# Seven small edits to the order of a decoder step: prefetch and scaling of x, a pinned subtraction, a store on another queue, a pause at the key head's change

## The chip, the cores and the metric

The program runs on one core of one Trainium2 chip. The metric is the time of one execution in microseconds on the device. A lower number is better.

## The reference

One inference step of a one-layer decoder with two groups of heads, for a prompt of 1024 tokens and eight further sequences of one token each (R = 1032 rows), all in float32:

```python
h = rmsnorm(x); p = project(h, w_in)          # 2048 wide; q, k, v, index q/k/w, gates, mLSTM q/k/v/i/f/o/z
att = dsa(p.q, p.k, p.v, p.qi, p.ki, p.wi)    # an indexer scores all keys, the 256 best are attended; 8 heads, 2 key heads
h_ml = mlstm(p.mq, p.mk, p.mv, p.ig, p.lf)    # gated linear recurrence, 4 heads, d_v 256, d_qk 128
a  = att * silu(p.az)
mo = rmsnorm_per_head(h_ml) * ml_norm_w * sigmoid(p.mo) * silu(p.mz)
y  = rmsnorm(x + concat(a, mo) @ w_out)
```

The eight further tokens read paged caches of 4096 earlier tokens through a page table (keys, values and index keys) and update stored mLSTM states. Returned are y for both parts, the new keys, values and index keys, and the mLSTM states.

## The kernel before

The matrix products are made of pairs of short floats: each operand is split into a high part H (a cast, on ACT) and a low part L (operand minus H, on DVE), and three products H·H, H·L and L·H are summed on TensorE (PE). So behind each weight tile stand a DMA load on SP, a cast on ACT (`wH`), a subtraction on DVE (`wL`), and PE.

The input projection walks over column blocks, numbered T = 0 to 60. T below 9 are the indexer's and other small parts, T = 9 to 16 the mLSTM values (line 1590), up to 36 the remaining ones (line 1520). From T_G = 37 the gates follow in pairs of column blocks (line 1757), as a Strassen scheme: quarters of x are summed in advance, into DRAM (`xsD`), and so are weights (`usD`). The output projection is again Strassen-like: a first part at line 2040, then sums of weight quarters and products at line 2107 (the tail of the program, from 1714 us on).

Beside the projections run side jobs, written as Python generators and handed out by three lanes. A job has an earliest start and a due time, both in units of T, and a weight, and each `yield w` says how much of the weight was done. The lane takes steps from a job so that it ends at its due time. `prep` makes the sums of x on POOL (`xsD`), `dscore` scores the cached index keys (it fetches rows `kp` by an indirect DMA on POOL, line 1001, and multiplies at line 1023), `att` is the attention of the prompt, `ml` the mLSTM.

The order on each engine comes from a planner that orders the instructions after a model of their times. An instruction that is wrapped in `pin` keeps its place in the program's order; `tc.high_priority()` lets one go ahead; all others may be moved within their dependencies. So a change of a job's due time reorders PE, DVE, ACT and SP over long stretches. Each engine's queue, and each engine's queue of DMA issues, works in order.

The names at the seven places:

- `job_att`: `load_k` loads the transposed keys of a key head into `kL` (line 583, from `akS`), ACT casts `kH` (584), DVE subtracts (585); in the trace these two tiles are named xL and xH. `scores` are the products at 637, `values` those at 681 and 690, `split_q` prepares queries. There are two key heads with 16 pairs of query blocks each; between the 16th and the 17th the key head changes.
- `job_ml`: `main` computes two heads of a chunk of 128 tokens (lines 843 to 920; products of CH with qH and qL at 892), `tail` transposes their rows on PE, copies them to `hT` (one buffer, line 930) and stores them to `hS` (line 931). `load` brings `rb` (831) and `qkv` (834).
- `job_prep`: for each of 16 steps `load` brings four quarters of x (1397), two multiplications for each of two halves scale them (1408 by the norm's weight `nw`, 1409 by `rstd`), three subtractions and an addition make the sums (1412 to 1415), two DMAs store them (1416, 1417). All of it is pinned on POOL.
- The tail: `sP4`, `sP7`, `sP5`, `sP3` are split sums of the quarters `quad(k)` of the activations (2017 and 2018 make sH and sL, 2171 is the subtraction a22 - a11, 2288 the later one, quad(k)[1] - quad(k)[3]). `tsplit` makes wH and wL (2091, 2096), `tsum` sums weights on POOL or DVE (2101), `add` adds products to `yt` (2221).

Of the kernel before, what the change touches and what calls it, by code (L numbers as in the profile page):

```python
# [8 lines left out]
F32 = mybir.dt.float32  # L9
# [43 lines left out]
T_AZ = 53  # L53
NT = 61
T_PA = 55.5
T_PRE = 58
HR = R // 2
CS = HR // 2
NP = (NT - T_G) // 2
# [112 lines left out]
def body(tc, A, stop=None):  # L172
# [65 lines left out]
    def bank(n=512, dt=F32, parts=128):  # L238
        t = psg.tile([128, 512], F32, name="bank")
        return t  # L240
# [328 lines left out]
    def job_att():  # L569
# [4 lines left out]
        with tc.tile_pool(name="at", bufs=2) as pa:  # L574
# [131 lines left out]
            for n, pair in enumerate(pairs):  # L706
                g, i, hp = pair
                nxt = pairs[n + 1] if n + 1 < len(pairs) else None
                ga, gb = groups(pair)
                now["oT"] = bank()  # L710
                if nxt:
                    if nxt[0] != g:
                        load_k(nxt[0])
                    if nxt[2] == 0:
                        split_q(*pre)
                        if n + 3 < len(pairs):
                            pre = load_q(*blocks[(n + 1) // 2 + 1])
                    new = start()
                    scores(nxt, 0, new)
                values(pair, now, ga)  # L720
                if nxt and nxt[0] != g:
                    vt = load_v(nxt[0])
                yield cost[n]
                if nxt:
                    scores(nxt, 1, new)
                    soft(nxt, new)
                values(pair, now, gb)
                V.reciprocal(cur["rc"][:, hp * 2:hp * 2 + 2, i], now["sv"][:, :, 3])
                ob = pa.tile([128, 2, 128], F32, name="ob", bufs=1)
                SC.copy(ob, now["oT"][:, :256].rearrange("p (a b) -> p a b", a=2))  # L730
                SY.dma_start(attS[g].rearrange("(j p) r -> p j r", p=128)[:, hp * 2:hp * 2 + 2, i * 128:(i + 1) * 128],
                             ob)
                if nxt is None or nxt[0] != g:
                    p = bank()
                    PE.transpose(p[:32, :128], cur["rc"].rearrange("p h i -> p (h i)"), ident)
                    rt = pa.tile([128, 512], F32, name="pP", bufs=6)[:32, :128]
                    V.tensor_copy(rt, p[:32, :128])
                    SY.dma_start(rcS[g].rearrange("h (i p) -> (h i) p", p=128), rt)
                if nxt:
                    if nxt[0] != g:  # L740
                        split_v(vt)
                    now = new
                yield cost[n]
# [67 lines left out]
    def job_ml():  # L811
        gT = mlc["gT"]
        with tc.tile_pool(name="ml", bufs=2) as pm:
# [109 lines left out]
            def tail(c, h0, hms):  # L923
                tsl = slice(c * 128, (c + 1) * 128)
                pH = bank().rearrange("p (a b) -> p a b", a=4)
                for hh in range(2):
                    for x in range(2):
                        PE.transpose(pH[:, hh * 2 + x, :], hms[hh][:, x * 128:x * 128 + 128], ident)
                hT = pm.tile([128, 4, 128], F32, name="hT", bufs=1)
                SC.copy(hT, pH)  # L930
                SY.dma_start(hS.rearrange("(j p) r -> p j r", p=128)[:, 2 * h0:2 * h0 + 4, tsl], hT)

            steps = [(c, h0) for c in range(8) for h0 in (0, 2)]
            ld = [load(*steps[0])]
# [454 lines left out]
    def job_prep():  # L1389
        with tc.tile_pool(name="sx", bufs=2, side="right") as px:  # L1390
            halves = rstd.rearrange("p (h t) -> p h t", h=2)
            steps = [(k, c) for k in range(8) for c in range(0, HR, CS)]

            def load(k, c):
                X = px.tile([128, 2, 2, CS], F32, name="X")
                for y in (1, 0):
                    pin(G.dma_start(X[:, y], A["xT"][k + 8 * y].rearrange("p (h t) -> p h t", h=2)[:, :, c:c + CS]))
                return X

            Xs = [load(*steps[0])]  # L1400
            yield 1
            for n, (k, c) in enumerate(steps):
                X = Xs.pop(0)
                if n + 1 < len(steps):
                    Xs.append(load(*steps[n + 1]))
                a11, a21, a12, a22 = (X[:, y, h] for y in range(2) for h in range(2))
                for y in (1, 0):
                    pin(G.tensor_scalar(X[:, y], X[:, y], nw[:, k + 8 * y:k + 8 * y + 1], None, OP.mult))
                    pin(G.tensor_tensor(X[:, y], X[:, y], halves[:, :, c:c + CS], OP.mult))
                yield 1  # L1410
                O = px.tile([128, 3, CS], F32, name="O")
                pin(G.tensor_tensor(O[:, 0], a21, a22, OP.subtract))
                pin(G.tensor_tensor(O[:, 2], a11, a21, OP.subtract))
                pin(G.tensor_tensor(O[:, 1], O[:, 0], a11, OP.subtract))
                pin(G.tensor_tensor(a12, a12, O[:, 1], OP.add))
                pin(G.dma_start(xsD[2:5, k, :, c:c + CS].rearrange("n p t -> p n t"), O))
                pin(G.dma_start(xsD[0:2, k, :, c:c + CS].rearrange("n p t -> p n t"), X[:, 1]))
                yield 1
# [34 lines left out]
    def ix_weight(blocks):  # L1453
# [5 lines left out]

    lanes = [Lane([Job("gates", 5, T_MV - 0.5, 8500, job_gates),  # L1460
                   Job("index", T_MV, 32.5, 3000 + sum(map(ix_weight, groups)), lambda: job_index(groups)),
                   Job("att", T_MQ, T_G + 11.5, 2 * 2 * sum(2 * (1 + (i + 1) * 0.5) for i in range(8)) + 14, job_att, att_free),
                   Job("ml", T_G + 8, T_PRE - 0.75, 39, job_ml)]),
             Lane([Job("prep", 3, T_MV + 5.5, 1 + 16 * 2, job_prep),
                   Job("dscore", T_MV + 6, 21.5, 24 + 128 + 2, job_dscore),
                   Job("dsel", T_MV, 30.5, 2000 + 31 * 1700 + 10000 + 16 * 2800 + 2000, job_dsel),
                   Job("qrows", T_MQ + 0.5, 31, 1, job_qrows),
                   Job("datt", T_MQ, T_G + 0.5, 10000 + 8 * 5000 + 34000 + 5 * 2500 + 8000 + 8000 + 5000, job_datt, ix_free),
# [806 lines left out]
    for n in range(2):  # L2275
        ps = banks3(n)
        for k in range(8):
            with tc.high_priority():
                b22 = wblock(1, 2 + n, k, pt, 6)
                b12 = wblock(0, 2 + n, k, *((wst, 2) if k % 2 else (pt, 6)))  # L2280
                T_ = tsplit(tsum(b22, b12, G), None, True)
            blocks(ps, k, sP7[k], T_, LOW)
            spread(3)
            if not n:
                with tc.high_priority():
                    sP5[k] = ssplit(quad(k)[2])
            if n:
                V.tensor_tensor(quad(k)[1], quad(k)[1], quad(k)[3], OP.subtract)
        for b in LOW:
            late.append(add(yt[b + HB][2 + n], ps[b], yt[b][2 + n]))  # L2290
            late.append(add(yt[b + HB][n], ps[b], yt[b + HB][n]))
        rows3(resid, HIGH, n, False)
        rows3(square, HIGH, n)
        rows3(resid, LOW, 2 + n, False)
        rows3(scaled, HIGH, n)
# [121 lines left out]
```

## Time and profile before

| | |
|---|---|
| median of three runs | 1970.5 us (1966.37 to 1972.38) |
| profiled execution | 1974.54 us, span of its instructions 1972.7 us |
| mean granted clock of TensorE | 0.993 |
| busy: PE, PEld, DVE, ACT, POOL | 1917.7, 1820.3, 1433.6, 900.2, 508.5 us |
| DMA | 421.31 MB, mean 214 GB/s |

The busy times are shares of the span of one execution; PEld is the loading of weights into TensorE, which runs beside the products. Stages by time: 0 to 176 us loading and the first columns, 176 to 390 the mLSTM values, 390 to 932 the columns up to T = 36, 932 to 1617 the gates, then the output projection until the end. A granted clock below 1 means that TensorE was slowed for a while.

### The profile page before, as it was taken

To read this page: it belongs to the slowest core of one execution; us is meant where nothing else is said; L and a number is where in the kernel's file an instruction comes from. 1 tells how busy PE (TensorE), PEld (TensorE's weight loads), DVE (VectorE), ACT (ScalarE), POOL (GpSimd) and SP (SyncE) were. 2 spreads that over 40 slices of the span, in tenths; PEclk is the share of its full clock that TensorE was granted. 3 is DMA by queue.
4 is the path that set the end of the run, shared out by engine and by line. 5 is a ranking of instruction groups with operands and counts; after the bars stand their busy time and mean duration, and the time that the engine had idled before them with its cause. 6 is when DMAs were issued, how large, how long until landed. Compare 5 with 4: busy or idle time off the path is not lost.

```text
span 1972.7 us, 35929 instructions
## 1 busy us (share of the span) xinstructions
PE 1917.7 (97%) x12710; PEld 1820.3 (92%) x12710; DVE 1433.6 (73%) x3280; ACT 900.2 (46%) x1864; POOL 508.5 (26%) x566
## 2 busy tenths in 40 slices
PE   9999999999999999999999999999999999998997
PEld 9998877899999999999999999999999999976885
DVE  8443878676868878975556658777778676788786
ACT  8122554445314454311345546555656434454545
POOL 0576777022311011042000000002123221106633
PEclk9999999999999999999999999999999999999999
DMA  7567556456998687575533687759789858898875
GB/s 262 143 201 201 168 170 186 119 143 199 261 250 228 176 210 209 136 223 191 162 98 113 210 282 207 239 181 280 226 279 316 216 204 291 265 322 284 267 239 187
DMA packets 250289, 421.31 MB, mean 214 GB/s; under 512 B 40101, under 2 KB 117221, under 8 KB 246269
## 3 DMA queue, kind: packets, MB, share of 16 engines
q1 hardware_dynamic: 217709, 328.80, 53.1%
q0 software_dynamic: 18432, 82.15, 15.7%
q10 hardware_dynamic: 13968, 8.06, 1.4%
q8 instruction: 100, 1.64, 0.4%
q14 instruction: 80, 0.66, 0.1%
HBM read 333.76 MB, written 135.48 MB: 238 GB/s over the span
## 4 chain that ended last, share of the span: by engine, by line
PE 75%; DMA 10%; DVE 8%; issue 3%; ACT 2%; SPq 1%; POOL 1%; ACTq 0%; POOLq 0%; DVEq 0%
PE pj L1520 24%; PE pj L1757 18%; PE pj L2107 5%; PE bank L2040 4%; PE bank L1757 3%; PE bank L489 3%; PE bank L637 2%; PE bank L690 2%; PE pj L1590 2%; PE bank L1520 2%; PE bank L681 1%; PE bank L1023 1%; DMA wraw<-in_wv_dram 1%; DVE wL L2096 1%; DMA spD<-ev 1%
## 5 line engine op out<-in xcount | busy, mean ns | idle before, releaser
L1520 PE MATMUL pj<-xH,wH 128*128 128x344 f32 (+1 forms) x1200 | 388.6, 326 | 5.3 <-DVE ev L375 1.9
L1520 PE MATMUL pj<-xH,wL 128*128 128x344 f32 (+1 forms) x1200 | 388.4, 324 | 1.2 <-DVE wL L252 1.2
L1520 PE MATMUL pj<-xL,wH 128*128 128x344 f32 (+1 forms) x1200 | 388.3, 324 | 0.2 <-DVE xL L309 0.2
L1757 PE MATMUL pj<-xH,xL 128*128 128x258 f32 x1152 | 328.1, 285 | 0.0
L1757 PE MATMUL pj<-xH 128*128 128x258 f32 x1152 | 327.9, 285 | 0.0
L1757 PE MATMUL pj<-xL,xH 128*128 128x258 f32 x1152 | 327.8, 285 | 0.0
L1520 PEld LDWEIGHTS pj<-xH,wH 128*128 128x128 f32 x1200 | 225.8, 189 | 8.6 <-issue 2.8
L1520 PEld LDWEIGHTS pj<-xH,wL 128*128 128x128 f32 x1200 | 226.1, 188 | 2.5 <-DVE wL L252 1.5
L1520 PEld LDWEIGHTS pj<-xL,wH 128*128 128x128 f32 x1200 | 226.0, 188 | 1.6 <-DVE xL L309 0.4
L251 ACT CAST wH<-wraw 128x512 fp32r<-128x512 f32 (+2 forms) x183 | 109.6, 610 | 258.3 <-PE pj L1520 161.5
L1757 PEld LDWEIGHTS pj<-xL,xH 128*128 128x128 f32 x1152 | 218.2, 189 | 1.3
L1757 PEld LDWEIGHTS pj<-xH 128*128 128x128 f32 x1152 | 218.3, 190 | 1.0 <-issue 0.4
L1757 PEld LDWEIGHTS pj<-xH,xL 128*128 128x128 f32 x1152 | 218.1, 190 | 1.0
L252 DVE TENSOR_TENSOR wL<-wraw,wH 128x512 fp32r<-128x512 f32 (+2 forms) x183 | 129.0, 715 | 74.4 <-ACT wH L251 71.9
L538 ACT ACTIVATE eq<-eq 128x512 bf16<-128x512 bf16 (+2 forms) x93 | 78.5, 844 | 129.5 <-DVE eq L537 129.2
L2107 PE MATMUL pj<-wL,sH 128*128 128x512 f32 x336 | 127.0, 397 | 8.2 <-DVE wL L2096 8.2
L2107 PE MATMUL pj<-wH,sH 128*128 128x512 f32 x336 | 132.5, 395 | 1.3 <-ACT wH L2091 1.1
L2107 PE MATMUL pj<-wH,sL 128*128 128x512 f32 x336 | 131.7, 392 | 0.0
L491 ACT ACTIVATE rl<-bank 128x512 f32<-128x512 f32 (+2 forms) x160 | 80.5, 524 | 97.7 <-PE bank L489 50.1
L494 DVE SCALAR_TENSOR_TENSOR s<-rl,wiN,s 128x512 f32<-128x512 f32 (+2 forms) x150 | 100.4, 689 | 21.2 <-ACT rl L491 18.8
L882 POOL CAST aH<-onec 128x4 fp32r<-128x4 f32 x16 | 5.5, 343 | 405.8 <-DVE onec L821 405.8
L2107 PEld LDWEIGHTS pj<-wL,sH 128*128 128x128 f32 x336 | 63.7, 190 | 24.2 <-DVE wL L2096 11.0
(511 smaller groups left out, 4817.9 us busy)
## 6 DMA issues: line engine op xcount, KB each, us to landing
wraw<-in_wt_dram SPq DMA_DIRECT2D x144, 256.0 KB
wraw<-in_wa_dram SPq DMA_DIRECT2D x110, 256.0 KB
usD<-in_wa_dram POOLq DMA_DIRECT2D x48, 512.0 KB, 7.6
wraw<-in_wo_dram SPq DMA_DIRECT2D x64, 256.0 KB
usD<-in_wa_dram SPq DMA_DIRECT2D x24, 512.0 KB
usD<-usD POOLq DMA_DIRECT2D x24, 512.0 KB, 5.9
xL<-xsD SPq DMA_DIRECT2D x40, 258.0 KB
ev<-spD SPq DMA_DIRECT2D x38, 258.0 KB
```

Of the source, the lines that this page charges most:

```text
L251: a = SC.copy(H[:, s, :cols], raw[:, s, :cols])
L252: return a, V.tensor_tensor(L[:, s, :cols], raw[:, s, :cols], H[:, s, :cols].bitcast(F32), OP.subtract)
L489: PE.matmul(p[:, :cn], qi[:, h % 4, :], ki[x][:, c0:c0 + cn], start=(x == 0), stop=(x == 1))
L491: SC.activation(r[:, :cn], p[:, :cn], AF.Relu)
L494: v = V.scalar_tensor_tensor(s[:, c0:c0 + cn], r[:, :cn], wv, s[:, c0:c0 + cn], OP.mult, OP.add)
L538: SC.activation(junk2[:, :W1], junk2[:, :W1], AF.Copy, accum_out=cnt[:, 1:2])
L637: PE.matmul(p[:, :cn], a_[:, h, :], b_[:, x, :cn], start=(z == 0), stop=(z == 2))
L690: PE.matmul(oT[:, :256], a_[:, k2 + kk, :], b_[:, ks_], start=(k2 + kk == 0 and z == 0), stop=(k2 + kk == i and z == 2))
L1520: m = PE.matmul(ps[:cols, :cn], w_[:, k, :cols], x_[kk][:, c0:c0 + cn], start=(kk == ends[0] and z == 0), stop=(kk == ends[1] and z == 2))
L1757: PE.matmul(ps[c], w_[:, q, ks], x[y][:, c * CS:c * CS + CS], start=(first and q == 0 and k == 0 and z == 0), stop=(q == 1 and k == 3 and ...
L2040: PE.matmul(banks[t], w_[:, k, :], x_, start=(q + k + z == 0), stop=(q == 3 and k == 3 and z == 2), skip_group_check=True)
L2107: PE.matmul(ps[b], S_[x][:, b * 128:b * 128 + 128], T_[y], start=(k == 0 and z == 0), stop=(k == 7 and z == 2))
```

## The change

Seven edits:

1. `T_PRE`, the time from which the last stage's pools may open and which sets the due time of `ml` (T_PRE - 0.75), goes from 58 to 58.5.
2. In `job_att`, at the change of the key head, the loading of the next key head and the first half of the value products of the last pair come first; then the lane pauses for 4 units; then the queries are split and the next scores computed. The job's weight grows from 222 to 226.
3. In `tail` of `job_ml` the store of hT is issued by ACT in place of SP.
4. In `job_prep` X has three buffers in place of two and is loaded two steps ahead in place of one; O has one buffer in place of two; the scaling by `nw` becomes a two-operand multiplication with a broadcast operand.
5. `prep` is due at T = 13.2 in place of 14.5; `dscore` may start at 13.7 in place of 15 and is due at 20.5 in place of 21.5.
6. The weights of `att` follow edit 2.
7. The later subtraction in the tail is pinned to its place in the program.

```diff
-T_PRE = 58
+T_PRE = 58.5
@@ job_att
                 now["oT"] = bank()
+                change = nxt and nxt[0] != g
+                if change:
+                    load_k(nxt[0])
+                    values(pair, now, ga)
+                    yield 4
                 if nxt:
-                    if nxt[0] != g:
-                        load_k(nxt[0])
                     if nxt[2] == 0:
                         split_q(*pre)
...
                     new = start()
                     scores(nxt, 0, new)
-                values(pair, now, ga)
-                if nxt and nxt[0] != g:
+                if change:
                     vt = load_v(nxt[0])
+                else:
+                    values(pair, now, ga)
                 yield cost[n]
@@ job_ml, tail
-                SY.dma_start(hS.rearrange("(j p) r -> p j r", p=128)[:, 2 * h0:2 * h0 + 4, tsl], hT)
+                SC.dma_start(hS.rearrange("(j p) r -> p j r", p=128)[:, 2 * h0:2 * h0 + 4, tsl], hT)
@@ job_prep
-                X = px.tile([128, 2, 2, CS], F32, name="X")
+                X = px.tile([128, 2, 2, CS], F32, name="X", bufs=3)
...
-            Xs = [load(*steps[0])]
+            Xs = [load(*steps[n]) for n in range(2)]
...
-                if n + 1 < len(steps):
-                    Xs.append(load(*steps[n + 1]))
+                if n + 2 < len(steps):
+                    Xs.append(load(*steps[n + 2]))
...
-                    pin(G.tensor_scalar(X[:, y], X[:, y], nw[:, k + 8 * y:k + 8 * y + 1], None, OP.mult))
+                    w = nw[:, k + 8 * y:k + 8 * y + 1].unsqueeze(2).to_broadcast([128, 2, CS])
+                    pin(G.tensor_tensor(X[:, y], X[:, y], w, OP.mult))
                     pin(G.tensor_tensor(X[:, y], X[:, y], halves[:, :, c:c + CS], OP.mult))
                 yield 1
-                O = px.tile([128, 3, CS], F32, name="O")
+                O = px.tile([128, 3, CS], F32, name="O", bufs=1)
@@ lanes
-                   Job("att", T_MQ, T_G + 11.5, 2 * 2 * sum(2 * (1 + (i + 1) * 0.5) for i in range(8)) + 14, job_att, att_free),
+                   Job("att", T_MQ, T_G + 11.5, 2 * 2 * sum(2 * (1 + (i + 1) * 0.5) for i in range(8)) + 18, job_att, att_free),
...
-             Lane([Job("prep", 3, T_MV + 5.5, 1 + 16 * 2, job_prep),
-                   Job("dscore", T_MV + 6, 21.5, 24 + 128 + 2, job_dscore),
+             Lane([Job("prep", 3, T_MV + 4.2, 1 + 16 * 2, job_prep),
+                   Job("dscore", T_MV + 4.7, 20.5, 24 + 128 + 2, job_dscore),
@@ the tail
-                V.tensor_tensor(quad(k)[1], quad(k)[1], quad(k)[3], OP.subtract)
+                pin(V.tensor_tensor(quad(k)[1], quad(k)[1], quad(k)[3], OP.subtract))
```

How this moves instructions, at three places. Line numbers of the changed program are larger by 4 from line 710 on and by 5 from line 1400 on.

DVE in the tail, before (some 1780 us into the run). L2171 and L2288 are the two subtractions of a quarter, L2018 makes the low part of an activation, L2096 that of a weight; the number behind a tells the tiles apart:

```order
L2288 TENSOR_TENSOR a_19699<-a_19699 128x384
L2096 TENSOR_TENSOR wL<-bank,wH 128x512
L2018 TENSOR_TENSOR sL<-a_19699,sH 128x384
L2018 TENSOR_TENSOR sL<-a_19746,sH 128x384
L2096 TENSOR_TENSOR wL<-bank,wH 128x512
L2171 TENSOR_TENSOR a_19746<-a_19746,a_18925 128x384
L2288 TENSOR_TENSOR a_19746<-a_19746 128x384
L2096 TENSOR_TENSOR wL<-bank,wH 128x512
```

The same quarters after the change (L2176, L2101 and L2023 are the former L2171, L2096 and L2018):

```order
L2023 TENSOR_TENSOR sL<-a_19699,sH 128x384
L2023 TENSOR_TENSOR sL<-a_19746,sH 128x384
L2101 TENSOR_TENSOR wL<-bank,wH 128x512
L2176 TENSOR_TENSOR a_19746<-a_19746,a_18925 128x384
L2101 TENSOR_TENSOR wL<-bank,wH 128x512
```

And a hundred rows later on DVE, among the rows that ran at 1875 to 1893 us before:

```order
L2293 TENSOR_TENSOR a_19746<-a_19746 128x384
L2101 TENSOR_TENSOR wL<-bank,wH 128x512
L2226 TENSOR_TENSOR yt_19963<-pj_21001,yt_19962 128x512
L2226 TENSOR_TENSOR yt_19581<-pj_21001,yt_19581 128x512
L2226 TENSOR_TENSOR yt_19967<-pj_21002,yt_19966 128x512
L2293 TENSOR_TENSOR a_19607<-a_19607 128x384
```

The eight later subtractions have moved out of the stretch of the first splits into the stage in which the program writes them.

SP's queue in the mLSTM before, around the store of one hT (it ran at 1460 us):

```order
L1799 DMA xL<-rcS_109 128x516
L1744 DMA wL<-usD 128x512
L1776 DMA ev<-spD 128x516
L931 DMA hS<-hT 128x4x128
L1799 DMA rstd<-rcS_108 128x508
L831 DMA rb<-rowS 128x512
```

ACT's queue after the change, at such a store:

```order
L876 CAST CH<-C 128x516
L882 CAST aH<-qkv 128x2x256
L934 COPY hT<-bank 128x512
L935 DMA hS<-hT 128x4x128
L916 ACTIVATE hn,st<-bank,st 128x256
L1750 CAST xH<-wL 128x512
```

The sixteen stores have left SP and stand behind their copies on ACT, mostly directly, at some with one or two other rows between.

SP's queue at the second key head before; L583 is its load, L1744 loads weights of the gates whose cast on ACT stands directly ahead of and behind the key's:

```order
L1707 DMA xL<-xsD 128x516
L583 DMA xL<-akS_99 128x2x512
L1744 DMA wH<-usD 128x512
L615 DMA qL<-aqS_104 128x4x128
L731 DMA attS_106<-ob 128x2x128
```

After:

```order
L583 DMA xL<-akS_99 128x2x512
L1242 DMA out_C_s_dram<-Cb 128x512
L615 DMA qL<-aqS_104 128x4x128
L735 DMA attS_106<-ob 128x2x128
L1781 DMA ev<-spD 128x516
L1744 DMA wL<-usD 128x2x512
L1712 DMA xL<-xsD 128x516 x4
L1242 DMA out_C_s_dram<-Cb 128x512
L1224 DMA Cb<-in_sC_dram 128x512
L1749 DMA wH<-usD 128x512
```

The key load now stands well ahead of the load of the weight tile wH (L1749, before L1744) that ACT casts next to it. PE's first product of `dscore` (L1023) has moved in the same way: behind products of the mLSTM values that ran at about 345 us before, where the first one before ran at 400 us.

## The prediction

> **What bounds the kernel now.** I read, in this order, the page's busy times, the windows by stage, the waits of PE, and then the timeline around each place where PE loses more than a microsecond.
>
> ```profile
> PE 1917.7 (97%) x12710; PEld 1820.3 (92%) x12710; DVE 1433.6 (73%) x3280; ACT 900.2 (46%) x1864; POOL 508.5 (26%) x566
> ...
> 176.00:390.00 214.00, 198.68 (x963) 173.71 (x962) 158.63 (x340) 96.67 (x230) 122.28 (x119) 0.99 0.59 171
> ...
> 932.00:1617.00 685.00, 676.20 (x5503) 667.32 (x5497) 478.45 (x1304) 357.02 (x798) 75.56 (x144) 1.00 0.70 216
> ...
> 1714.00:1972.70 258.70, 236.88 (x1022) 191.46 (x1020) 210.31 (x338) 134.12 (x269) 103.16 (x75) 0.97 0.77 262
> ```
>
> The columns of a window are its length, the busy times of PE, PEld, DVE, ACT and POOL, the granted clock, the DMA share and GB/s. TensorE bounds the program: it is idle for only 1972.7 - 1917.7 = 55 us. Its matmuls are the same before and after, so all that this change can give back is these 55 us and what the clock loses. 15.3 us of them lie in the window 176 to 390 (the v projection), 8.8 in the gate stage (932 to 1617) and 21.8 in the output tail (from 1714). What PE waited for:
>
> ```profile
> PE pj L2107 <- DVE wL L2096: 8.2, 4, 5.0
> PE bank L1590 <- DVE wL L1586: 5.7, 7, 1.6
> PE bank L1590 <- ACT wH L1585: 4.5, 2, 3.1
> PE bank L637 <- ACT xH L584: 2.7, 1, 2.7
> PE bank L489 <- ACT rl L491: 2.4, 2, 1.4
> PE bank L892 <- ACT qH L825: 2.2, 1, 2.2
> PE bank L892 <- DVE qL L826: 1.6, 1, 1.6
> ```
>
> Total, times, longest, all in us. Three of these waits are touched by the change: L2107 (the tail), L637 (attention, at the key head's change) and L892 (mLSTM). A second loss follows some waits: the granted clock.
>
> ```profile
> 294.00:310.00 16.00, 12.89 (x56) 11.22 (x55) 13.24 (x36) 7.34 (x18) 9.48 (x10) 0.89 0.67 198
> 1452.00:1485.00 33.00, 29.19 (x224) 28.77 (x224) 21.91 (x54) 15.05 (x36) 9.76 (x15) 0.90 0.98 340
> 1782.00:1815.00 33.00, 26.59 (x107) 20.59 (x106) 28.20 (x38) 13.56 (x26) 22.37 (x16) 0.95 0.73 251
> ```
>
> A mean clock of 0.90 over 33 us is 0.10 x 33 = 3.3 us lost at PE, 0.95 is 1.65 us, and 0.89 over 16 us is 1.8 us. So a stall of several us is paid again afterwards. The Trainium skill ("TensorE: Matmul & The Clock Gate", Part 1) says that the clock halves after an idle window of about 3.4 us; half speed for 3.4 us would be 1.7 us, as the rows at 294 and 1782 have it, but the row at 1452 shows two such losses after waits of 2.2 and 1.6 us, shorter than the page's window.
>
> **The later subtractions (tail).** The eight subtractions of L2288 are now queued on DVE far ahead of their place in the program, in the stretch where PE waits longest:
>
> ```profile
> L2288 DVE TENSOR_TENSOR a<-a x8: 548/1034/1684, 1763.8 to 1802.1; 128x384 f32<-128x384 f32 x8
> 1756.00:1803.00 47.00, 40.59 (x169) 32.20 (x168) 46.79 (x64) 25.59 (x53) 21.90 (x16) 0.96 0.74 249
> 1875.00:1893.00 18.00, 18.00 (x81) 14.89 (x81) 15.61 (x26) 12.22 (x26) 7.58 (x5) 1.00 0.62 207
> 1786.95 0.68 DVE L2096 TENSOR_TENSOR wL<-bank,wH 128x512 fp32r<-128x512 f32 x1
> ...
> 1788.14 1.68 DVE L2288 TENSOR_TENSOR a<-a 128x384 f32<-128x384 f32 x1
> ...
> 1789.75 3.18 DVE L2018 TENSOR_TENSOR sL<-a,sH 128x384 fp32r<-128x384 f32 x2
> ...
> 1792.85 0.68 DVE L2096 TENSOR_TENSOR wL<-bank,wH 128x512 fp32r<-128x512 f32 x1
> ...
> 1794.50 1.51 DVE L2288 TENSOR_TENSOR a<-a 128x384 f32<-128x384 f32 x1
> 1795.93 0.68 DVE L2096 TENSOR_TENSOR wL<-bank,wH 128x512 fp32r<-128x512 f32 x1
> ...
> 1796.67 1.65 PE L2107 MATMUL pj<-wL,sH 128*128 128x512 f32 x3 [5.02 <-DVE wL L2096]
> ```
>
> From 1756 to 1803 DVE is busy for 46.79 of 47 us: there, every DVE instruction ahead of a low part wL delays PE. By the order, seven of the eight subtractions come before the wL of 1795.93 and all leave that stretch. The two in the timeline alone took 1.68 + 1.51 = 3.2 us; the others took at least 0.55 each, so 5 x 0.55 = 2.7 more, together 5.9 us at least and 7 x 1.03 = 7.2 at the median. PE's waits for wL at L2107 are 8.2 us, nearly all here. I take 6.0 us of wait removed and the 1.65 us of clock with it: -7.6. The lower end is -5 (the low part would also be held by the wH that ACT makes), the upper -8.2 - 1.65 = -9.9. In their new place, among the rows that ran at 1875 to 1893, DVE is busy for 15.6 of 18 us and PE lost nothing; eight subtractions bring 8 x 0.55 = 4.4 to 8 x 1.03 = 8.2 us, more than the 2.4 us of room. What covers them is that wL runs ahead of PE there; I charge 0.5 us (0 to 4). Net -7.1.
>
> **The key head's change.** Now ACT, in order, meets the cast of the second key head while its load is still under way:
>
> ```profile
> 1136.38 0.58 SPq L583 DMA_DIRECT2D xL<-akS  x1
> ...
> 1144.39 1.04 ACT L584 CAST xH<-xL 128x1024 fp32r<-128x1024 f32 x1 [6.79 <-DMA xL<-akS]
> ...
> 1145.49 0.44 PE L637 MATMUL bank<-xH,qH 128*128 128x128 f32 x2 [2.70 <-ACT xH L584]
> ```
>
> The load takes 8 us from issue to cast and PE waits 2.70. After the change the load is issued ahead of the first value products, and the lane pauses for four units before the scores that need it. The lane's 226 units (208 for the costs + 18) are due over the first 11.5 column steps of the gate stage, which take 685 / 24 = 28.5 us each (the window above), so four units are 11.5 x 28.5 x 4 / 226 = 5.8 us: enough for a 2.7 us shortfall. -2.5 (-2.7 to 0). ACT still stands at the cast in order; behind it are the next weight cast and ptH, but nine issues of SP now lie between the key load and the load of that next weight tile, so ACT meets the cast later relative to the load. The lane's later parts get four units less time, about 2%; nothing in the rows reads as bound by that: 0.
>
> **The mLSTM row store.** This is the chain at the worst place of the gate stage:
>
> ```profile
> 1443.59 0.58 ACT L930 COPY hT<-bank 128x512 f32<-128x512 f32 x1
> ...
> 1460.76 0.37 SPq L931 DMA_DIRECT2D hS<-hT  x1
> ...
> 1466.75 0.58 ACT L930 COPY hT<-bank 128x512 f32<-128x512 f32 x1 [4.99 <-DMA hS<-hT]
> ...
> 1467.95 0.38 PE L892 MATMUL bank<-CH,qH 128*128 128x258 f32 x1 [2.23 <-ACT qH L825]
> ...
> 1469.39 0.17 DVE L843 COPY dk<-rb 128x2 f32<-128x2 f32 x1 [1.40 <-DMA rb<-rowS]
> ...
> 1470.28 0.58 PE L892 MATMUL bank<-CH,qL 128*128 128x258 f32 x1 [1.58 <-DVE qL L826]
> ```
>
> hT has one buffer. It was full at 1444.2, but SP, which issues in order, reached its store only at 1460.76; ACT's next copy waited 4.99 us for that store to land and held up ksH and qH behind it, and PE waited. Issued by ACT right behind the copy, the store starts 16 us earlier and lands long before. That takes 2.23 us for certain. The 1.58 us for qL has another part: dk waits for the row load rb. SP is now one issue shorter there (0.37 us), but DMA was at 0.98 of its time between 1452 and 1485, so rb can stay late. Gain between -2.2 and -(2.23 + 1.58 + 3.3) = -7.1; I take -5.0, since without the first wait the second alone would seldom cost both clock losses. The price: sixteen issues on ACT of about 0.4 us (SP's row above: 0.37), 6 us of an engine that is busy 357 of 685 us here. Where ACT is early, as before most of PE's needs, this is hidden: 0 (0 to +1).
>
> **Preparation of x, its due time, and dscore.** POOL's side:
>
> ```profile
> L1408 POOL TENSOR_SCALAR X<-X,nw x32: 1566/1602/2108, 70.3 to 334.8; 128x516 f32<-128x516 f32 x32
> L1409 POOL TENSOR_TENSOR X<-X,rstd x32: 1191/1203/1619, 72.0 to 336.7; 128x516 f32<-128x516 f32 x32
> POOL X L1397 <- DMA xsD<-X: 67.8, 13, 8.5
> L1001 POOL DMA_INDIRECT kp<-in_cik_dram,idx x32: 940/981/1432, 367.1 to 528.1; - x32
> DMA to landing us min/median/max: 3.3/3.7/14.1
> L1023 PE MATMUL bank<-bd,kp x256: 270/275/276, 400.4 to 540.9; 128*128 128x128 f32 x128
> ```
>
> The scaling by nw becomes the operation of L1409, at the same shape: 32 x (1602 - 1203) ns = 12.8 us of POOL less. The third X buffer does not remove the wait of L1397: the load for two steps ahead still reuses the buffer whose store was issued an instruction before it. What goes is that wait at the end, since the last loads come a step earlier (about one, 67.8 / 13 = 5 us). The single O buffer is rewritten after four multiplications, 4 x 1.2 = 4.8 us, against a store that takes about as long: 0 to 0.5 us a step, hidden behind the X wait. So POOL ends the preparation near 342 - 13 - 5 = 324 instead of about 342. PE does not wait for that by itself: 0. But it is needed now, since the key fetches of dscore stand behind it on POOL, and PE's first L1023 has moved in order from 400.4 to the neighbours that ran at about 345. Fetch at 326, landing after 3.7 (at worst 14.1): 330 to 340, so 5 to 15 us to spare. I charge +0.5.
>
> **The rest.** The job end T_PRE moves mLSTM and the opening of a pool by some 14 us; the first mixing loads there come after both: 0. PE, DVE and ACT get another order from 165 to 1600 us, because the planner goes by job times. Of this no row gives a sign. In the v projection the waits for wL and wH of L1590 (5.7 + 4.5) and their clock loss could go (about -10), or as many come; I take 0 there and +1 for new waits in a gate stage that lost only 8.8 us.
>
> Sum: -7.1 - 2.5 - 5.0 + 0.5 + 1 = -13.1 us. The profiled execution was 1974.5 (1.8 above its span), so it becomes 1961.4; it was 4.0 above the median of the three runs, so against 1970.5 I forecast **1957.4, say 1957.5**.
>
> **Rivals.**
> 1. *The preparation is late and PE stands at the first dscore product.* POOL's two-input operation took up to 1619 ns. If all 64 multiplications took that, they would need 32 x 0.017 + 32 x 0.416 = 13.9 us more instead of 12.8 less; without the saved wait, preparation ends at 356, the first key rows land at 361 to 371, and PE, due at 345, stalls 16 to 26 us and pays 1.7 for the clock. It decides against the change from a stall of about 17 us on (13.1 gained + 5.9, less the clock): 1970.5 - 13.1 + 27 = 1984 at the far end, about 1979 in the middle. Against it: the median of 32 such operations is 1203. The Trainium skill ("GPSIMD Engine Reference", 3.1 and 4.1) speaks for it: an operation with two inputs takes about 2.6 cycles an element and one with one input about 1. By its figures, as an estimate, the scaling would go from 0.44 to 1.12 us, the preparation would be 22 us longer and the result this rival's far end; the rows above, 1602 with one input and 1203 with two, contradict the page. Chance 0.06.
> 2. *The tail gives it back.* The subtractions need up to 8.2 us where 2.4 are free and push wL behind PE at 1880 to 1893: +4 and 1.7 for the clock, time 1963. Chance 0.13.
> 3. *Neither load nor store was the cause.* The DMA burst (0.98, 340 GB/s) delays rb and the key rows as before, so the second and third terms are only -2.2, and the new order adds 5 in the v projection beside the 1.5 charged above: 1970.5 - 7.1 - 2.2 + 6.5 = 1968. The change then does little beside its tail. Chance 0.16.
> 4. *The new order also smooths the v projection.* Half of its 15 us goes: 1949. Chance 0.12.
>
> **How the numbers follow.** My forecast has 0.53, its own range 1951 to 1963. A measurement of this kernel tells about 0.3% (5.9 us) from no change: faster means below 1964.6, slower above 1976.4. Faster: 0.50 of the forecast, 0.12 of rival 4, 0.09 of rival 2, 0.04 of rival 3: 0.75. Slower: 0.05 of rival 1, 0.02 of rival 3: 0.07. Same: 0.18. The range for 8 in 10 takes in most of rivals 2, 3 and 4 and leaves rival 1 out: 1946 to 1969.
>
> **What would show it.** Tail: the L2288 rows after 1860, no wait of PE at L2107 above 2 us around 1790, granted clock 1.00 there. Key head: L637's wait on ACT gone. Store: no ACT wait for hS at L930, L892's waits below 1.6 together, the clock at 1452 to 1485 at 0.95 or better. Preparation: scaling near 1.2 us, the last xsD store near 324, no PE wait at L1023. Wrong if L1023 waits for kp, or if PE's idle in 176 to 390 grows past 20 us.

## The result: slower by 1.3%, and the profile after

Six runs of the changed kernel have a median of 1994.2 us (1990.4 to 1999.95), six of before 1971.2. The ratio is 1.0126, with a 95% interval from 1.0105 to 1.0148: 25 us slower by that ratio, where 13 us less had been forecast and the range ended at 1969. The profiled execution took 1999.95 us, at the upper end of its runs. Its busy times on the page:

```profile
PE 1928.7 (97%) x12710; PEld 1826.5 (91%) x12710; DVE 1447.0 (72%) x3280; ACT 901.5 (45%) x1864; POOL 489.3 (24%) x566
```

Its windows by stage, same columns as before:

```profile
176.00:390.00 214.00, 190.58 (x891) 163.91 (x890) 162.91 (x328) 89.97 (x213) 116.31 (x123) 0.96 0.57 167
390.00:932.00 542.00, 526.99 (x3348) 514.55 (x3347) 413.68 (x1010) 199.02 (x390) 101.49 (x119) 0.99 0.70 190
932.00:1617.00 685.00, 679.23 (x5473) 667.93 (x5472) 470.99 (x1299) 352.19 (x786) 74.58 (x136) 1.00 0.71 218
```

PE idles 23.4 us in the v projection (15.3 before; more than 20 was one of the prediction's signs of being wrong) and 15.0 from 390 to 932 (2.3 before), and its clock in the v projection fell to 0.96. What it waited for (total, times, longest, in us):

```profile
PE pj L1525 <- DVE ev L375: 14.2, 2, 11.9
PE bank L1595 <- DVE wL L1591: 11.7, 6, 5.7
PE bank L1595 <- ACT wH L1590: 7.0, 4, 5.2
PE pj L2112 <- DVE wL L2101: 3.6, 2, 2.0
PE bank L896 <- ACT qH L829: 3.2, 1, 3.2
```

Windows at fixed times mix the stages once a program runs late. So I numbered the 10080 products of the five main lines (1520, 1590, 1757, 2040, 2107), which come in the same order in both kernels, and compared when product n starts:

| product | before, us | after, us | after later by |
|---|---|---|---|
| 1000 (v projection) | 204.5 | 204.6 | 0.1 |
| 1400 (its end) | 395.0 | 417.7 | 22.7 |
| 2600 | 642.5 | 656.6 | 14.1 |
| 3800 | 848.0 | 865.1 | 17.1 |
| 4000 | 883.1 | 913.5 | 30.4 |
| 5800 (gates) | 1207.0 | 1241.7 | 34.7 |
| 7000 | 1423.5 | 1448.9 | 25.4 |
| 7600 | 1526.5 | 1552.3 | 25.8 |
| 9200 (tail) | 1749.6 | 1778.3 | 28.7 |
| 9400 | 1803.9 | 1824.7 | 20.7 |
| 10000 | 1942.0 | 1968.0 | 26.0 |

The loss has two places: some 14 us in the v projection (of the 22.7, 8.8 are dscore's products, which now stand there and are missing later) and 13 us around 880. The windows give the same 14 for the first place: 8.1 us more idle time, and a clock of 0.96 in place of 0.99 over 214 us, which is 6.4 us. Between products 5800 and 7000 (the rest of the attention and the first mLSTM chunks) 9 us seem to be won, but 57 products of the side jobs have left that stretch, 23 for the stretch before it and 34 for those behind it, so most of this is work that moved. In the tail 8 us were won (9200 to 9400), of which 5 were lost again.

The stall at 880, in the changed kernel's timeline (SP, POOL, DVE, PE):

```profile
831.09 0.45 SPq L1162 DMA_DIRECT2D slotS<-rai  x1
...
838.57 0.48 SPq L980 DMA_DIRECT2D qrowS<-jk  x1
839.10 0.59 SPq L1432 DMA_DIRECT2D usD<-in_wa_dram  x1
...
844.54 1.58 POOL L1435 DMA_DIRECT2D usD<-in_wa_dram  x2 [70.03 <-issue]
...
880.35 0.77 POOL L1435 DMA_DIRECT2D usD<-in_wa_dram  x1 [9.68 <-DMA usD<-usD]
881.43 1.06 POOL L1293 DMA_INDIRECT ck<-in_ck_dram,idxs  x1 [0.31 <-DMA mlS<-ev]
...
886.15 1.23 DVE L1318 TENSOR_TENSOR jk<-ck,qb 128x1024 f32<-128x1024 f32 x1 [12.47 <-DMA ck<-in_ck_dram,idxs]
...
887.86 0.66 PE L1525 MATMUL pj<-xH,wH 128*128 128x344 f32 x1 [11.90 <-DVE ev L375]
```

And before:

```profile
781.70 0.62 SPq L1427 DMA_DIRECT2D usD<-in_wa_dram  x1
...
814.50 0.32 SPq L1158 DMA_DIRECT2D slotS<-rai  x1
...
845.15 1.73 POOL L1289 DMA_INDIRECT ck<-in_ck_dram,idxs  x1 [42.13 <-DVE pb L1269]
```

The last copy for the sums of weights (job `usum`, usD) was issued by SP at 781.70. Now it stands behind the end of the sample selection (slotS, qrowS) and leaves at 839.10. The selection itself did not come earlier: its slotS was issued at 814.50 before and is issued at 831.09 now. POOL works in order, so the last ten issues of the sums, chained through DRAM, run from 844 to 881, ahead of the gather of the cached keys that the next job wants. DVE, in order too, stands at the product with those keys for 12.47 us, and behind it is the eviction ev for which PE waits 11.90. The window there shows what the clock adds to it, 0.77:

```profile
870.00:900.00 30.00, 15.78 (x84) 15.24 (x83) 15.04 (x18) 1.50 (x3) 13.64 (x15) 0.77 0.85 237
```

### The profile page after: what moved, and what is told of

The parts are those of the page before. It is cut to its first block, busy times and chain, and to the rows that moved or that the text cites. A ratio compares the mean times of both kernels' runs of the same rounds, so it can differ in the third digit from the quotient of the medians.

```text
span 1998.2 us, 35912 instructions
## 1 busy us (share of the span) xinstructions
PE 1928.7 (97%) x12710; PEld 1826.5 (91%) x12710; DVE 1447.0 (72%) x3280; ACT 901.5 (45%) x1864; POOL 489.3 (24%) x566
## 3 DMA queue, kind: packets, MB, share of 16 engines
q0 software_dynamic: 18432, 82.15, 15.6%
## 4 chain that ended last, share of the span: by engine, by line
PE 74%; DVE 10%; DMA 9%; issue 3%; ACT 2%; SPq 1%; POOL 0%; ACTq 0%; DVEq 0%; POOLq 0%
PE pj L1525 24%; PE pj L1762 18%; PE pj L2112 6%; PE bank L2045 4%; PE bank L1762 3%; PE bank L489 3%; PE bank L637 2%; PE bank L690 2%; PE bank L1525 2%; PE bank L1027 1%; PE bank L681 1%; PE bank L896 1%; PE pj L1600 1%; DVE wL L1591 1%; PE pj L1595 1%
## 5 line engine op out<-in xcount | busy, mean ns | idle before, releaser
L1435 POOL DMA_DIRECT2D usD<-in_wa_dram x48 | 41.7, 914 | 235.0 <-DMA usD<-in_wa_dram 88.5
```

What stands on the lines that cost most here:

```text
L1435: return lambda: G.dma_start(usD[n, i], src, accum_op=OP.add, max_dma_last_dim=8192)
```

## The experiments

Eleven kernels, each timed against before on the same chip in three rounds (e9 in five). Ratios are to before; e5 to e8 ran on another chip than the others, so kernels are compared by these ratios. Each has one profiled execution, which the product numbers are taken from.

**e1: the pin alone.** `pin(...)` around the later subtraction, nothing else.

> Only the later subtraction is pinned. If the tail's DVE queue is what held PE there (the prediction's first term), 6 to 8 us less than before, about 1964, the L2288 rows after 1860 and PE's waits for wL at L2107 down from 8.2 to about 3.6, as in the changed kernel. If the eight subtractions only move the wait to their new place, within 2 us of before.

Measured: 0.9985 (0.9965 to 1.0005), about -3 us and not clear of zero. The row of the subtractions:

```profile
L2288 DVE TENSOR_TENSOR a<-a x8: 542/550/1614, 1870.0 to 1890.8; 128x384 f32<-128x384 f32 x8
```

The window of the tail and PE's wait there:

```profile
1756.00:1803.00 47.00, 45.87 (x200) 36.97 (x199) 42.77 (x62) 27.79 (x57) 24.27 (x17) 1.00 0.84 283
```

```profile
PE pj L2107 <- DVE wL L2096: 3.9, 3, 2.5
```

The mechanism is as read: they moved, DVE is no longer full (42.77 of 47 us, 46.79 before), and the longest wait is 2.5. But in four other kernels whose tail is that of before, the same wait is 5.9 to 6.4 in sum, not the 8.2 of the one profiled execution; against 3.9 that is 2 to 2.5 us won. The product numbers of all profiles agree. From 9200 to 9400 the five kernels without the pin take 4.8 us more in the mean than the eight with it, but from 9400 to 10000, where the subtractions now stand, they take 3.2 us less. Some 1.6 us are left: 190.3 to 192.4 us for both stretches without the pin, 187.5 to 191.2 with it.

**e2: the store alone.**

```diff
-                SY.dma_start(hS....[:, 2 * h0:2 * h0 + 4, tsl], hT)
+                SC.dma_start(hS....[:, 2 * h0:2 * h0 + 4, tsl], hT)
```

> Only the mLSTM row store is issued by ACT. By the prediction: -5 us, about 1965.5. By the trace of the changed kernel, where ACT itself stood 6.4 us at one such store until the transfer of a weight tile had landed and PE then waited 3.2 us for qH: one wait replaced by another, between -2 and +3 us, and a store on ACT that starts several us after its copy.

Measured: 1.0043 (1.0023 to 1.0063), 8.5 us slower, more than either expected. ACT in e2's timeline:

```profile
1455.41 0.59 ACT L930 COPY hT<-bank 128x512 f32<-128x512 f32 x1 [0.54 <-DMA wH<-usD]
1463.72 0.37 ACTq L931 DMA_DIRECT2D hS<-hT  x1
1464.18 1.05 ACT L1740 CAST xH<-wH 128x1024 fp32r<-128x1024 f32 x1 [8.18 <-DMA qkv<-mlS]
```

PE's wait in e2:

```profile
PE bank L892 <- ACT qH L825: 5.6, 1, 5.6
```

The copy is done at 1456.0 and the store leaves only at 1463.72. In the instruction list (of e2, copy and store) the store waits for two things: its copy (Activation), and a numbered completion counter (DMAHW1). The program has eight such counters for the transfers that SP and ACT issue, and an issue first waits until the transfer that used its counter before has landed.

```
L930 COPY hT<-bank 128x512 [waits DMAHW1_49,PE_49]
L931 DMA hS<-hT 128x4x128 [waits DMAHW1_49,Activation_49]
```

Here that was SP's row load rb, issued at 1456.71: the trace has the last of its signals on this counter at 1463.64, and the store leaves 0.08 us later (the row above names another load of that time, qkv). In the changed kernel it was a load of wL for the gates, and the next instruction of ACT had to wait 6.41 us:

```profile
1479.86 0.37 ACTq L935 DMA_DIRECT2D hS<-hT  x1
1480.27 0.47 ACT L916 ACTIVATE hn<-bank,st 128x256 bf16<-128x256 f32 x1 [6.41 <-DMA wL<-usD]
```

On SP such a wait holds up loads. On ACT it holds up every cast, and PE waits 5.6 us for one, against 2.23 + 1.58 before. By product number e2 falls 6 us behind between 1457 and 1527; but 32 products of the mLSTM, which before has later, run in that stretch, and at product 9200 the two are level (1750.3 and 1749.6). The profiled execution of e2 (1974.58) is below the median of its runs and that of before (1974.54) above, so the profiles show the wait, but not where all of the 8.5 us are lost.

**e3: the scaling alone**, `tensor_scalar` by nw replaced by `tensor_tensor` with a broadcast.

> Only the scaling of x becomes a two-operand multiplication with a broadcast. Theory A (due times are the cause of all the loss): POOL's scaling 1.6 to 1.06 us, time as before within 3 us. Theory B (two-operand work of POOL slows DVE's small instructions in the v projection): 6 to 12 us more than before, PE's idle time between 176 and 420 us grows by as much, and DVE's mean durations there grow.

Measured: 1.0040 (1.0024 to 1.0056), 8 us slower: theory B. The product numbers put the loss into the v projection: from product 1000 to 1400, without dscore's products, the nine kernels with the one-operand scaling take 187.8 to 192.1 us, e3 takes 200.3, and the three others with two operands, which also have the prefetch, 204.3 to 205.8. Three of the nine (e4, e6, e11) have the earlier due times, so those cost nothing there. In the changed kernel the operation itself became faster than forecast, 1054 ns:

```profile
L1413 POOL TENSOR_TENSOR X<-X,nw x32: 1041/1054/2029, 72.1 to 317.3; 128x516 f32<-128x516 f32 x32
L1414 POOL TENSOR_TENSOR X<-X,rstd x32: 1185/1407/2073, 73.2 to 318.6; 128x516 f32<-128x516 f32 x32
```

POOL's wait before a load of X, in the changed kernel:

```profile
POOL X L1401 <- DMA xsD<-X: 69.6, 13, 8.6
```

But the scaling slows DVE. The subtraction wL of the v projection takes 663 to 670 ns (means of each kernel) where POOL does nothing; where POOL's one-operand scaling covers more than half of it, 672 to 808 (nine kernels, 8 to 14 cases each); beside the two-operand scaling, 1037 to 1167 (four kernels, 4 to 6 cases each). Summed over all of DVE's instructions from 66 to 400 us, the time above the median of the same line and shape without POOL beside it is 38 to 46 us in the nine and 48 to 57 in the four: some 9 us more in the mean. DVE's small instructions, which are in a chain with ACT (bisection for the selection), show it too. The copy at L547 takes 0.16 us alone, at most 0.64 beside the one-operand scaling and 0.91 to 0.97 beside the two-operand one. The largest case in the changed kernel stands beside the multiplication by rstd, which has two operands in both kernels; the second row is the same instruction with no multiplication beside it:

```profile
296.65 1.17 DVE L547 COPY_PREDICATED im<-im 128x2 int32<-128x2 int32 x1
...
303.40 0.16 DVE L547 COPY_PREDICATED im<-im 128x2 int32<-128x2 int32 x1
```

The Trainium skill ("GPSIMD Engine Reference", section 8) says that GPSIMD shares its SBUF interfaces with VectorE and contends with DVE instructions that have two SBUF inputs; wL has two, and agrees. Its rule that an operation with two inputs takes GPSIMD longer than one with one input (sections 3.1 and 4.1) does not fit: 1054 against 1602 ns.

**e4: the due times of prep and dscore alone.**

```diff
-             Lane([Job("prep", 3, T_MV + 5.5, ...),
-                   Job("dscore", T_MV + 6, 21.5, ...),
+             Lane([Job("prep", 3, T_MV + 4.2, ...),
+                   Job("dscore", T_MV + 4.7, 20.5, ...),
```

> Only the due times of prep and dscore are earlier. Theory A: the last weight-sum copy stands behind the end of the sample selection on SP, POOL's last sums and so the key gather are late, and PE stands 10 to 14 us for ev at L375 near 880 us; the v projection loses some 10 us too: +20 to +25, about 1993. Theory B: the stall at 880 is there, the v projection loses nothing: +12 to +15, about 1985.

Measured: 1.0123 (1.0095 to 1.0151), +24 us, in size the upper expectation. These two numbers alone cost as much as the whole change. The last usD copy leaves SP at 826.36, behind qrowS at 825.82, the wait for ev at L375 is 7.9 us, and the clock from 880 to 900 is 0.83. By product number 18 of the 24 us fall between 816 and 946 of before's time, nearly all at this stall (products 3800 to 4000, 46.0 us in place of 35.1) and at a second one (4200 to 4400, 38.5 in place of 29.9, clock 0.83 from 950 to 960), whose cause is not shown. The v projection lost nothing, against the expected 10 (187.8 us from product 1000 to 1400 without dscore's, 190.5 before); in the trace stands a wait of 1.8 us for kp. By the instruction lists of kernels with one of the two due times (not timed), neither alone puts the copy behind slotS; it takes both.

**e5: the changed kernel with usum due earlier.**

```diff
-             Lane([Job("usum", 19, T_G - 4, 8 * NP, job_usum)])]
+             Lane([Job("usum", 19, T_G - 6, 8 * NP, job_usum)])]
```

> The changed kernel with the sums of weights (usum) due two columns earlier, so that their last copies stand ahead of the end of the sample selection on SP. If that late copy is what makes POOL's sums, then the key gather, then ev, then PE late: PE's waits for ev at L375 fall from 14.2 us to about 2, the clock near 880 is back at 0.95 or more, and the time falls by 12 to 18 us against the changed kernel, to about 1978 to 1982. If the selection itself is what is late, the wait stays and the time is within 3 us of the changed kernel.

Measured: 1.0081 (1.0052 to 1.0110), 9 us less than the changed kernel; the profiled execution, 1978.4, is at the low side of its runs (median 1986). The one wait left for ev at 870 is 1.85 us, and the window there is at full clock:

```profile
860.00:900.00 40.00, 38.15 (x243) 37.90 (x242) 34.09 (x54) 3.72 (x6) 18.12 (x18) 1.00 0.73 217
```

The last usD copy leaves SP at 756.16, ahead of slotS at 820.92, and the key gather starts at 860.85 (881.43 in the changed kernel). So the late copy was the cause of that stall. All thirteen profiles fit: products 2600 to 4000 take 256.9 to 257.9 us in the three kernels with both earlier due times and usum as before (changed, e4, e6), 238.8 to 243.7 in the ten others. The gain by the ratios is below the expected 12 to 18. The v projection's loss is still there (22.5 us late at product 1600, as in the changed kernel).

**e6: the changed kernel with the scaling as before.**

> The changed kernel with the scaling by nw as before (one operand), all else kept. If POOL's two-operand work slows DVE and with it the v projection: 6 to 10 us less than the changed kernel, about 1986, DVE's extra time beside POOL down by some 10 us. Rival: the longer preparation (0.4 us more in each of 32 operations) makes dscore's first product wait for its keys and gives the gain back: within 3 us of the changed kernel, with a wait for kp at L1023.

Measured: 1.0097 (1.0064 to 1.0130), some 6 us less than the changed kernel (the intervals overlap). In its profile the v projection's loss is gone: product 2600 comes at 641.0 us, against 656.6 in the changed kernel and 642.5 before. The stall at 880 has stayed, and e4's second stall is here too (39.0 us for products 4200 to 4400, 32.0 in the changed kernel), which takes back 7 of these 16 us. PE's wait for kp at L1027 is 0.5 us, so the longer preparation does not hold up dscore.

**e7: before with the pause and the pin.**

> Before with only the pause at the key head's change and the pinned subtraction. By the terms as the runs now size them: -3 for the pin and -2.7 to -3.5, some clock with it, for PE's wait at L637: about 1962 to 1964. Rival: the pause moves the lane's later parts and costs as much as the wait: 1966 as with the pin alone.

Measured: 0.9972 (0.9947 to 0.9998), 5.5 us faster, 2.5 more than the pin alone, though the two intervals overlap. ACT hardly waits at the second key head any more, and L637 is gone from PE's waits (2.7 to 3.7 us in all kernels without the pause):

```profile
1134.25 1.06 ACT L584 CAST xH<-xL 128x1024 fp32r<-128x1024 f32 x1 [0.60 <-DMA xL<-akS]
```

**e8: before with the store issued by POOL** (`G.dma_start`).

> Before with the mLSTM row store issued by POOL in place of SP. If the loss with ACT came from ACT standing at the store until an unrelated transfer was done, POOL, which has little to do here, can stand instead: ACT's 5.0 us wait for hS gone, PE's wait for qH at L892 gone, -2 to -5 us against before, about 1966. Rival: the transfers themselves are late in this burst and whatever queue issues the store, ACT or DVE waits for it or for rb: within 2 us of before.

Measured: 0.9973 (0.9949 to 0.9996), 5.3 us faster. PE's wait for qH is gone, and the clock from 1452 to 1485 is 1.00 (0.90 before). 2.6 us for ksL is what is left there. ACT still waits for two stores (the last row shown of the view of hS lists who waited for it), but at 1544 and 1559, and PE is busy without a gap from 1470 to 1560:

```profile
L931 POOL DMA_DIRECT2D hS<-hT x16: 763/826/888, 1359.6 to 1560.7; - x16
...
  ACT hT L930: 11.5, 2
```

And PE's wait in the mLSTM:

```profile
PE bank L898 <- DVE ksL L868: 2.6, 1, 2.6
```

Sixteen issues of 0.83 us on POOL show no cost. The same store is worth -5 us on POOL and +8.5 on ACT.

**e9: the three that gain: pause, pin, store on POOL.**

> Before with the pause at the key head's change, the pinned subtraction, and the store of the mLSTM rows on POOL. If the three are independent: 0.9972 x 0.9973 = 0.9945 of before, about 1960, PE without waits at L637 and with at most 3 us at L892. If the pause and the store shift the same waits into each other, between 0.997 and 1.000.

Measured: 0.9935 (0.9914 to 0.9956): 1960.9 against 1971.7, faster than both kernels. What the three give when they are independent, 0.9945, lies within the interval. Its busy times:

```profile
PE 1916.0 (98%) x12710; PEld 1819.3 (93%) x12710; DVE 1431.5 (73%) x3280; ACT 902.3 (46%) x1864; POOL 521.2 (27%) x582
```

The window of the gates, and PE's wait in the tail:

```profile
932.00:1617.00 685.00, 678.91 (x5525) 670.33 (x5524) 478.75 (x1308) 360.07 (x800) 90.29 (x160) 1.00 0.70 216
```

```profile
PE pj L2111 <- DVE wL L2100: 3.6, 4, 1.5
```

No wait of PE at L637 or L896 is left in the list.

**e10: the changed kernel with the old due times.**

> The changed kernel with the due times of prep and dscore as before, all else kept. If the due times cost what they cost alone (+1.2%) and the rest adds up (store on ACT +0.4%, scaling +0.4%, pin with pause -0.3%): +0.5%, about 1980, no wait above 2.5 us for ev at L375. If the loss of the due times needs the other edits, within 3 us of the changed kernel.

Measured: 1.0054 (1.0035 to 1.0073): as the parts add up. PE's wait for qH at L896 is 5.0 us, the v projection still idles (188.82 of 214 us busy), as the two-operand scaling is still there.

**e11: the changed kernel with three repairs:** store on POOL, scaling with one operand, usum two columns earlier.

> The changed kernel with three repairs: the store on POOL in place of ACT, the scaling with one operand, usum due two columns earlier; due times, prefetch, pause and pin kept. If the three name all of the loss: the changed kernel's +1.26% less 0.45 (usum), less 0.29 (scaling), less 0.7 (store) gives about -0.2%, 1964 to 1970. If earlier due times cost the v projection by themselves: +0.3% or more, above 1976, with PE's idle time between 176 and 420 us above before's.

Measured: 0.9975 (0.9960 to 0.9990), 5 us faster than before and within the expected 1964 to 1970 (1966.7). So these three repairs undo the whole loss. Against e9 it is still 0.4% slower, and the intervals do not overlap; it differs from e9 by the earlier due times, usum's due time, the prefetch and T_PRE. By product number 3.8 us of this have come by product 2600 (PE is busy for 194.03 of 214 us in the v projection, 197.86 in e9), and 8.3 by product 9200.

## Why the prediction was wrong

| part | forecast, us | measured |
|---|---|---|
| pin in the tail | -7.1 | -3 alone (e1, -7 to +1); -1.6 in the tail of all profiles |
| pause at the key head | -2.5 | -2.5 (e7 less e1, not clear of zero) |
| store on ACT | -5.0 | +8.5 alone (e2) |
| scaling, two operands | 0 | +8 alone (e3), 6 in place (e6) |
| due times, with the new order | +1.5 | +24 alone (e4), 14 in place (e10) |

- **The due times** are the step that failed worst. The prediction followed `prep` and `dscore` themselves, and there its ends were right: preparation ended at 325 (324 forecast), and PE hardly waited for kp (0 in the changed kernel, 1.8 in e4). It did not ask what the other jobs issue beside them. In the new order the last copy of usum, a job of another lane, stands behind the end of the selection in SP's queue, where it stood ahead of it; the late copy was the head of a chain on POOL, DVE and PE. The orders that it quoted stood at the three places that the edits aim at, and none at this one. Giving the reordering 0 in the v projection and +1 in the gate stage, because "of this no row gives a sign", was the mis-sized term: with the +0.5 for dscore it was +1.5, and it measured 14 in place and 24 alone. Rivals 2 and 3 let the tail give back some of its gain and let the new order add 5 us in the v projection, but no rival had one job's transfer fall behind another job's end.
- **The scaling**: the gain on POOL was right in kind (1.6 to 1.06 us) and worthless, as said. One reason is in no sentence of the prediction: the first fetch of dscore waits for DVE, which makes its indices, and not for the preparation. In e3 the preparation ended 14 us earlier than before (328.7 against 342.7), and the fetch began at 366.6 against 367.1; in the changed kernel it began at 340.5, not at the forecast 326, after POOL had waited 15.6 us for DVE. The step that failed is the price of 0. That two-operand work on POOL costs DVE was in the trace of before (DVE's wL beside L1409) and was not priced. Rival 1 had POOL's two-operand operation as its subject but a late preparation as its mechanism; that did not happen (e6, e10).
- **The third X buffer** did not remove the wait, as forecast: POOL's wait at the load was 67.8 us and is 69.6. With it the preparation ended 4 us earlier (324.8 against 328.7 in e3; 338.9 in e6 against 342.7 before), where 5 was forecast.
- **The store**: the reading of the wait (store late on SP, ACT's copy behind it) was right, as e8 shows. The step that failed is "issued by ACT right behind the copy". In this program an issue waits for a completion counter as well, and that wait came along to the queue on which every cast of the stage stands. Moving an issue was priced as 0.4 us of issue each.
- **The pin**: right in mechanism, but at least twice too large. One profiled execution was taken for the usual size (8.2 us of wait there, 5.9 to 6.4 in four others), and the new place of the subtractions was charged 0.5 us where the profiles show 3.2; there rival 2 was right in kind.
- **The key head**: the wait of L637 went, as forecast; the 2.5 us agree with the forecast but are within the noise of the two runs. The prediction counted nine issues of SP between the key load and that of wH (L1749); its list has eleven.

The parts add to 35 us alone and 25 together. e10 fits their sum without the due times (0.43 + 0.40 - 0.28 = 0.55% against 0.54% measured), so it is the due times that cost less when the other edits are there: 0.72% in place of 1.23%. In the profiles part of that is the second stall, which e4 has (38.5 us for products 4200 to 4400) and the changed kernel hardly (32.0, against 29.9 before). Why is not settled, nor how the 0.4% between e9 and e11 splits between the due times, usum, the prefetch and T_PRE; the last two were not timed alone.

## What to carry to other kernels

When the due time of a job is moved, list what every in-order queue issues at the end of that job and of its successors, and what the jobs of the other lanes issue at that time, in both orders: a single transfer that falls behind another job's end can cost more than the edit was to gain. Before an issue is moved to another engine, look at everything the issue waits for and put it on the engine that can best afford to stand; here POOL, not ACT. Before work on POOL is made faster, look at what DVE pays for its second operand.

## What the runs showed of the hardware

- A multiplication of 128x516 floats took POOL 1602 ns (median of 32, before) with a per-partition scalar and 1054 ns (changed kernel) with a broadcast tensor operand.
- DVE's subtraction of two SBUF operands (128x480 and 128x512) took 0.67 us alone, 0.67 to 0.81 beside POOL's one-operand operation and 1.04 to 1.17 beside the two-operand one (means by kernel); a predicated copy of 128x2 elements went from 0.16 to 0.97 us beside the two-operand scaling, and to 1.17 beside the multiplication by rstd.
- The same wait (PE for wL in the tail, in kernels with the same tail) was 8.2 us in one execution and 5.9 to 6.4 in four others: a term read from a single profile carries such an error.
- In the trace of before, TensorE's granted clock is 0.5 for 3.41 us from 857.8, 6.83 us from 1468.8 and 3.41 us from 1741.8. In the 3.41 us ahead of each of the three, PE was busy for 44%, 33% and 48% of the time, after single waits of 1.9, 2.2 and 1.8 us.
